# First loads on three queues, constant products ahead of them, and the memory norm behind the first convolution block

## The chip, the core and the metric

The kernel runs on one core of one Trainium2 chip. The metric is the device time of one execution in microseconds (us). The engines are named as in the profile: PE is TensorE (matmuls; PEld is its weight load), DVE VectorE, ACT ScalarE, POOL GpSimd, SP SyncE, which issues most of the transfers.

## What is computed

A model of width 1024 on 512 tokens: a layer with a short convolution, a layer with windowed attention, both with attention to a memory of 256 rows and a gated feed-forward part, and a third block behind them. What the change touches is the beginning of the first layer, cut here from the reference:

```python
def rmsnorm(x, g):
    x32 = x.astype(jnp.float32)
    y = x32 * lax.rsqrt(jnp.mean(x32 * x32, axis=-1, keepdims=True) + EPS)
    return (y * g.astype(jnp.float32)).astype(x.dtype)
...
    mem_n = rmsnorm(mem, mem_norm)
...
        mem_kv = mem_n @ w_mem_kv[i]
        mk, mv = jnp.split(mem_kv, 2, axis=-1)
...
        h = rmsnorm(x, norm_mix[i])
...
            proj = h @ a_w_in[i]
            u, b_gate, c_gate, q_mem = jnp.split(
                proj, [CONV_WIDTH, 2 * CONV_WIDTH, 3 * CONV_WIDTH], axis=-1)
            y_tok = _short_conv(u, b_gate, c_gate, a_conv_w[i])
```

`_short_conv` multiplies `c_gate` with `u`, filters that with three taps along the tokens and multiplies the result with `b_gate`.

## The kernel before, in words

Activations are held with the 1024 features on partitions, as eight chunks of 128 x 512. Every fp32 operand of a product is split into a high part (ScalarE copies it, L70) and a low part (VectorE subtracts, L76 for activations with their gain, L80 for weights), and a product is three matmuls (`mm3`): high by high (L120), low activation by high weight (L121), high activation by low weight (L122). `weights` fetches one block of 128 columns, 512 KB, as `wr`, and splits it into `wh` and `wl`; the first two blocks are fetched, and split, in two halves. There are two `wr` buffers and three each of `wh` and `wl`, so a block's fetch waits until the block two ahead has been split.

The root mean square of a token is one factor per column of the result, so the products begin before it is known: `g` is the chunk times its gain, and the factor `R` is multiplied onto the result. For it ScalarE squares the chunks (`sq`), VectorE adds them up (`acc`), `token_mean` sums over partitions with matmuls on ones (L174), VectorE works out the reciprocal root in a dozen small dependent steps (`m`, `ri`, `rt`, `rz`), and `spread` builds diagonals `dg` (L203) and multiplies them with ones on TensorE (L206) to have the factor on all partitions (`Ra`).

`load_consts` issues the first transfers. The first layer (`layer_a`) then runs convolution block 0 (products `u` and `c` in bank group `pp`, `b` in `lg`), block 1 (`lg`, `lg`, `po`), then `mem_kv`: `mem_rows` fetches the eight memory chunks, squares them, forms `mrs` and `mR` in the manner of `R`, and splits `gm`; two products for keys and the products for values follow. Behind them stand the queries, whose first product (L120 into `pp`) is the first `pp` product after the blocks; then the memory attention and blocks 2 to 5.

Each engine executes its own instructions strictly in order, and so does each queue that issues transfers. That order is set by the framework's scheduler when the kernel is built, from the order of the code and its own estimates of cost. `sink` (twelve numbers for the second layer) is fetched here and negated on VectorE (`negsink`).

## Time and profile before

| | |
|---|---|
| three runs | 1681.52, 1681.77 and 1689.32 us, median 1681.77 |
| the profiled execution | 1686.65 us, its span 1684.9 us |
| mean granted clock of TensorE | 0.987 |
| busy: PE, DVE, ACT, POOL | 1619.6, 1248.2, 756.6, 196.4 us |
| moved by DMA | 171.60 MB |

The span reaches from the first to the last instruction. Times within it count from its start. Starts in a timeline are those of instructions, which overlap: on TensorE the distance from start to start is the pace, not the length given. "[1.64 <-ACT wh L70]" says that the engine stood idle for 1.64 us before the instruction and that ScalarE's write of `wh` ended that. The granted clock is in parts of full speed.

### The profile page before, as it was taken

How to read it: one execution, taken by the hardware profiler on the slowest of the kernel's cores; microseconds unless marked ns; L12 is line 12 of the kernel's file. 1: busy time of each engine (PE TensorE's matmuls, PEld its weight loads, DVE VectorE, ACT ScalarE, POOL GpSimd, SP SyncE). 2: the span in 40 equal slices, each digit the busy share in tenths (PEclk: the TensorE clock that was granted, in tenths of full speed). 3: DMA queues.
4: the chain of work that ended last, by engine and by line, in shares of the span. 5: the costliest groups of instructions: out<-in, count | busy, mean ns of one | idle time of the engine just before them, and what ended most of it. 6: DMA issues, size and time to landing. Idle time of an engine off the chain costs nothing.

```text
span 1684.9 us, 24388 instructions
## 1 busy us (share of the span) xinstructions
PE 1619.6 (96%) x9408; PEld 1415.5 (84%) x9408; DVE 1248.2 (74%) x2330; ACT 756.6 (45%) x1404; POOL 196.4 (12%) x186
## 2 busy tenths in 40 slices
PE   8999999999999699999999999979999999999997
PEld 6887888999999588888889999857788888888887
DVE  7866788787776869877877777579788977764443
ACT  6532244454445467634444444324556533333233
POOL 1112410000000600041000000151001000010010
PEclk9999999999999799999999999989999999999999
DMA  6222222332234522232233233332511122243342
GB/s 199 88 88 88 100 76 100 101 113 101 101 104 123 183 94 77 68 101 88 85 103 113 89 113 98 91 118 86 172 45 57 40 76 92 70 150 113 124 158 88
DMA packets 51572, 171.60 MB, mean 102 GB/s; under 512 B 6680, under 2 KB 6880, under 8 KB 51328
## 3 DMA queue, kind: packets, MB, share of 16 engines
q1 hardware_dynamic: 45504, 151.11, 27.1%
q0 software_dynamic: 5376, 18.82, 3.3%
q8 instruction: 74, 1.21, 0.3%
q14 instruction: 42, 0.34, 0.1%
q10 hardware_dynamic: 576, 0.11, 0.0%
HBM read 160.56 MB, written 11.81 MB: 102 GB/s over the span
## 4 chain that ended last, share of the span: by engine, by line
PE 71%; DVE 15%; DMA 7%; ACT 3%; issue 3%; POOL 1%; SPq 0%; DVEq 0%; ACTq 0%; POOLq 0%
PE pp L122 8%; PE pp L121 8%; PE pp L120 8%; PE lg L120 4%; PE lg L121 4%; PE lg L122 4%; DMA wr<-in_w_gu_dram 3%; DVE wl L80 3%; PE pp L575 3%; PE pp L576 2%; PE pp L577 2%; PE tp L262 2%; PE tp L120 2%; PE tp L121 2%; PE tp L122 2%
## 5 line engine op out<-in xcount | busy, mean ns | idle before, releaser
L70 ACT ACTIVATE wh<-wr 128x1024 fp32r<-128x1024 f32 (+3 forms) x246 | 251.9, 1025 | 371.7 <-PE pp L121 129.1
L80 DVE TENSOR_TENSOR wl<-wr,wh 128x1024 fp32r<-128x1024 f32 (+3 forms) x246 | 305.6, 1243 | 70.1 <-ACT wh L70 68.8
L122 PE MATMUL pp<-g,wl 128*128 128x512 f32 x592 | 235.0, 397 | 11.2 <-DVE wl L80 11.2
L120 PE MATMUL pp<-g,wh 128*128 128x512 f32 x592 | 235.8, 399 | 8.1 <-ACT wh L70 8.1
L121 PE MATMUL pp<-g,wh 128*128 128x512 f32 x592 | 234.1, 396 | 0.2 <-DVE g L76 0.2
L122 PEld LDWEIGHTS pp<-g,wl 128*128 128x128 f32 x592 | 112.2, 189 | 33.7 <-DVE wl L80 13.0
L120 PEld LDWEIGHTS pp<-g,wh 128*128 128x128 f32 x592 | 112.6, 190 | 30.3 <-ACT wh L70 8.9
L121 PEld LDWEIGHTS pp<-g,wh 128*128 128x128 f32 x592 | 112.4, 190 | 21.6 <-DVE g L76 0.9
L70 ACT ACTIVATE s<-s 128x512 fp32r<-128x512 f32 x136 | 85.0, 631 | 62.5 <-DVE s L555 59.7
L120 PE MATMUL tp<-acth,wh 128*128 128x512 f32 x264 | 104.4, 396 | 5.7 <-DVE x L638 3.3
L121 PE MATMUL tp<-actl,wh 128*128 128x512 f32 x264 | 104.0, 394 | 0.0
L122 PE MATMUL tp<-acth,wl 128*128 128x512 f32 x264 | 103.4, 392 | 0.0
L80 DVE TENSOR_TENSOR s<-s,s 128x512 fp32r<-128x512 f32 x136 | 90.3, 685 | 1.9 <-ACT s L70 1.7
L575 PE MATMUL pp<-Bh,s 128*128 128x256 f32 x272 | 77.5, 285 | 3.4 <-ACT g L70 3.4
L575 PE MATMUL lg<-Bh,s 128*128 128x256 f32 x272 | 77.8, 286 | 1.3 <-DVE u L582 1.3
L577 PE MATMUL pp<-Bh,s 128*128 128x256 f32 x272 | 77.4, 285 | 0.3
L577 PE MATMUL lg<-Bh,s 128*128 128x256 f32 x272 | 77.4, 285 | 0.0
L555 DVE TENSOR_TENSOR s<-wr,wr 128x512 f32<-128x512 f32 x68 | 46.8, 688 | 39.7 <-DMA wr<-in_w_gu_dram 39.7
L120 PEld LDWEIGHTS tp<-acth,wh 128*128 128x128 f32 x264 | 50.0, 190 | 16.4 <-ACT wh L70 2.6
L122 PEld LDWEIGHTS tp<-acth,wl 128*128 128x128 f32 x264 | 50.0, 190 | 10.6
L638 DVE TENSOR_TENSOR x<-x,tp 128x512 f32<-128x512 f32 x72 | 49.2, 683 | 12.6 <-PE tp L122 12.6
L576 PE MATMUL lg<-Bl,s 128*128 128x256 f32 x204 | 58.1, 285 | 0.0
(503 smaller groups left out, 4557.5 us busy)
## 6 DMA issues: line engine op xcount, KB each, us to landing
wr<-in_w_gu_dram SPq DMA_DIRECT2D x68, 512.0 KB, 3.8
wr<-in_w_in_dram SPq DMA_DIRECT2D x44, 512.0 KB, 3.5
wr<-in_w_down_dram SPq DMA_DIRECT2D x32, 512.0 KB, 3.7
wr<-in_a_w_in_dram SPq DMA_DIRECT2D x18, 512.0 KB, 3.5
wr<-in_w_down_dram SPq DMA_DIRECT2D x16, 384.0 KB, 3.3
wr<-in_w_gate_dram SPq DMA_DIRECT2D x10, 512.0 KB, 3.5
wr<-in_w_up_dram SPq DMA_DIRECT2D x10, 512.0 KB, 3.4
wr<-in_a_w_out_dram SPq DMA_DIRECT2D x8, 512.0 KB, 3.4
```

The source lines that it names most:

```text
L70: self.nc.scalar.activation(out, in_, AF.Copy, scale=scale)
L80: self.nc.vector.tensor_tensor(out, x, hi.bitcast(F32), op=ALU.subtract)
L120: mm(ps, ah, bh, start=start, stop=False)
L121: mm(ps, ah, bl, start=False, stop=False)
L122: mm(ps, al, bh, start=False, stop=stop)
L262: self.nc.tensor.transpose(ps[:, c:c + 128], src, self.ident)
L555: nc.vector.tensor_tensor(t, a, b, op=ALU.add)
L575: mm(ps, ah, bh, start=start and j == 0, stop=False, skip_group_check=not start)
L576: mm(ps, ah, bl, start=False, stop=False, skip_group_check=not start)
L577: mm(ps, al, bh, start=False, stop=j == 3, skip_group_check=not start)
L638: nc.vector.tensor_tensor(x, x, ps, op=ALU.subtract)
```

## The change

Chunks 4 to 7 of x are issued from GpSimd's queue and the second weight block from ScalarE's; the other first loads stay with SyncE. The fetch of `ident` is written further down. Ten fp32 matmuls of ones by ones (128 x 128) go into a bank of the group `tp`, and `zero` is made from their result times 0 in place of from `ones`. `mem_rows` is called between blocks 0 and 1, and its result is handed to `mem_kv`.

```diff
--- before.py
+++ after.py
@@ -100,7 +100,7 @@
         self.lo_of(lo[:, :n], x, hi[:, :n], scale)
         return hi, lo
 
-    def weights(self, src, nk, nn, parts=1):
+    def weights(self, src, nk, nn, parts=1, eng=None):
 
         nc, n = self.nc, nk * nn
         raw = self.wp.tile([128, 1120], F32, name=self.nm("wr"), tag="wr", bufs=self.wbufs["wr"])
@@ -108,7 +108,7 @@
         lo = self.wp.tile([128, WMAX], F32R, name=self.nm("wl"), tag="wl", bufs=self.wbufs["wl"])
         step = n // parts
         for s in (slice(a, a + step) for a in range(0, n, step)):
-            nc.sync.dma_start(raw[:, s], src[:, s] if parts > 1 else src)
+            (eng or nc.sync).dma_start(raw[:, s], src[:, s] if parts > 1 else src)
         for s in (slice(a, a + step) for a in range(0, n, step)):
             self.copy(hi[:, s], raw[:, s])
             self.lo_of(lo[:, s], raw[:, s], hi[:, s])
@@ -300,15 +300,20 @@
         self.ones = self.const("ones", [128, 128])
         nc.vector.memset(self.ones, 1.0)
         self.zero = self.const("zero", [128, 128], F32R)
-        self.copy(self.zero, self.ones, 0.0)
         nc.scalar.dma_start(self.gains, T["gains"])
-        nc.scalar.dma_start(self.ident, T["ident"])
         self.x = [self.slot("x", name="x") for _ in range(8)]
         nc.sync.dma_start(self.x[0], T["x"][:, 0])
+        for c in range(4, 8):
+            nc.gpsimd.dma_start(self.x[c], T["x"][:, c])
+        ps = self.psum("tp")[:, :128]
+        for i in range(10):
+            nc.tensor.matmul(ps, self.ones, self.ones, start=i == 0, stop=i == 9)
+        self.copy(self.zero, ps, 0.0)
         self.h0 = self.gained(self.x[:1], self.gain(0))
-        self.w0 = [self.weights(T["a_w_in"][i], 8, 128, 2) for i in (0, 12)]
-        for c in range(1, 8):
+        self.w0 = [self.weights(T["a_w_in"][i], 8, 128, 2, e) for i, e in ((0, nc.sync), (12, nc.scalar))]
+        for c in range(1, 4):
             nc.sync.dma_start(self.x[c], T["x"][:, c])
+        nc.scalar.dma_start(self.ident, T["ident"])
         self.conv = self.const("conv", [128, 18])
         nc.scalar.dma_start(self.conv, T["conv"])
         self.sink = self.const("sink", [128, 12])
@@ -369,9 +374,9 @@
             res.append((hi, lo))
         return res
 
-    def mem_kv(self, layer):
+    def mem_kv(self, layer, gm=None):
         nc, T = self.nc, self.T
-        gm = self.mem_rows()
+        gm = gm or self.mem_rows()
         ks = []
         for b in range(2):
             ps = self.psum("lg")[:, :256]
@@ -481,8 +486,9 @@
         h = self.h0 + self.gained(self.x[1:], self.gain(0)[:, 1:])
         _, R = self.norm_row(1e-5, "Ra", True)
         ys = [self.conv_block(0, h, R, "b", self.w0)]
+        gm = self.mem_rows()
         ys.append(self.conv_block(1, h, R, "b", banks=("lg", "lg", "po")))
-        ks, vs = self.mem_kv(0)
+        ks, vs = self.mem_kv(0, gm)
         qs = []
         for b in range(2):
             qs += self.stack_q(self.queries(T["a_w_in"][18 + b], h, R))
```

The scheduler then sets another order. ScalarE at the start of the program, before (`g` and `acc` are of the first x chunk, `wr_93` and `wr_102` the first two weight blocks):

```order
L304 DMA gains<-in_gains_dram 128x64
L70 ACT_TABLE_LOAD
L70 ACTIVATE zero<-ones 128x128
L305 DMA ident<-in_ident_dram 128x128
L70 ACTIVATE g_90<-x_81,gains 128x512
L313 DMA conv<-in_conv_dram 128x18
L70 ACTIVATE wh_94<-wr_93 128x512 x2
L315 DMA sink<-in_b_sinks_dram 128x12
L70 ACTIVATE wh_103<-wr_102 128x512 x2
L159 ACTIVATE acc_145<-x_81 128x512
```

and with the change (`wr_107` and `wr_116` are the two blocks, `tp_92` the bank of the constant products):

```order
L303 DMA gains<-in_gains_dram 128x64
L316 DMA ident<-in_ident_dram 128x128
L111 DMA wr_116<-in_a_w_in_dram 128x512 x2
L70 ACT_TABLE_LOAD
L70 ACTIVATE g_104<-x_79,gains 128x512
L70 ACTIVATE zero<-tp_92 128x128
L70 ACTIVATE wh_108<-wr_107 128x512 x2
L70 ACTIVATE wh_117<-wr_116 128x512 x2
L318 DMA conv<-in_conv_dram 128x18
L320 DMA sink<-in_b_sinks_dram 128x12
L70 ACTIVATE g_135<-x_80,gains 128x512
```

The fetches of the second block are new here, the fetches of `conv` and `sink` stand behind the splitting of both blocks, `ident` is still the second, and the table load stands directly ahead of `g`.

VectorE behind the splitting of the first block, before (`g` with its three operands is the low half of a chunk):

```order
L80 TENSOR_TENSOR wl_95<-wr_93,wh_94 128x512 x2
L80 TENSOR_TENSOR wl_104<-wr_102,wh_103 128x512 x2
L317 TENSOR_SCALAR negsink<-sink 128x12
L76 SCALAR_TENSOR_TENSOR g_124<-x_82,gains,g_124 128x512
L76 SCALAR_TENSOR_TENSOR g_127<-x_83,gains,g_127 128x512
L166 TENSOR_TENSOR acc_145<-acc_145,sq_147 128x512
L76 SCALAR_TENSOR_TENSOR g_130<-x_84,gains,g_130 128x512
```

and with the change:

```order
L80 TENSOR_TENSOR wl_109<-wr_107,wh_108 128x512 x2
L80 TENSOR_TENSOR wl_118<-wr_116,wh_117 128x512 x2
L76 SCALAR_TENSOR_TENSOR g_135<-x_80,gains,g_135 128x512
L76 SCALAR_TENSOR_TENSOR g_138<-x_81,gains,g_138 128x512
L322 TENSOR_SCALAR negsink<-sink 128x12
L76 SCALAR_TENSOR_TENSOR g_141<-x_82,gains,g_141 128x512
L76 SCALAR_TENSOR_TENSOR g_144<-x_83,gains,g_144 128x512
```

`negsink` has moved behind the first two low halves, and the adds of the squares behind all of the low halves.

TensorE in block 1, before (`lg_299` is its product `u`, `dg_193` the first norm's diagonals):

```order
L122 MATMUL lg_299<-g_133,wl_304 128x512
L120 MATMUL lg_299<-g_136,wh_303 128x512
L121 MATMUL lg_299<-g_136,wh_303 128x512
L206 MATMUL tp_198<-dg_193,ones 128x512
L122 MATMUL lg_299<-g_136,wl_304 128x512
L120 MATMUL lg_299<-g_139,wh_303 128x512
L121 MATMUL lg_299<-g_139,wh_303 128x512
```

and with the change, from the end of block 0 on (`lg_393` and `lg_394` are block 1's `u` and `c`, `tp_341` takes the memory's means):

```order
L122 MATMUL lg_215<-g_153,wl_275 128x512
L120 MATMUL lg_393<-g_104,wh_397 128x512
L121 MATMUL lg_393<-g_104,wh_397 128x512
L120 MATMUL lg_394<-g_104,wh_429 128x512
L121 MATMUL lg_394<-g_104,wh_429 128x512
L206 MATMUL tp_209<-dg_204,ones 128x512
L174 MATMUL tp_341<-ones,acc_318 128x2 x2
L122 MATMUL lg_393<-g_104,wl_398 128x512
L120 MATMUL lg_393<-g_135,wh_397 128x512
```

The spread product of the first norm stood behind 17 matmuls of block 1 and stands behind four now, and the memory's means follow at once, where they came behind the whole of block 1. The memory norm's own spread product now stands behind the third matmul of block 1's last product, `po`; before it stood in the products for the memory's keys and values.

## Rows read from the trace of the kernel before

**Rows 1.** The page, first part: busy us, share of the span and instructions by engine.
```profile
PE 1619.6 (96%) x9408; PEld 1415.5 (84%) x9408; DVE 1248.2 (74%) x2330; ACT 756.6 (45%) x1404; POOL 196.4 (12%) x186
```

**Rows 2.** Stretches: length, busy us by engine (count), granted clock, DMA share, GB/s.
```profile
55.70:59.00 3.30, 3.30 (x14) 3.12 (x15) 2.56 (x5) 1.60 (x4) 0.00 (x0) 0.50 0.72 259
571.00:588.00 17.00, 7.42 (x21) 6.23 (x22) 14.28 (x29) 3.52 (x5) 8.95 (x13) 0.50 0.60 215
```

**Rows 3.** DMA view, 0 to 20 us: 40 slices; issues: queue, count, KB, us to landing.
```profile
DMA  0005689999798999999999998898998997899972
GB/s 0 0 0 49 175 202 323 320 321 314 258 299 295 397 387 387 322 362 395 392 403 394 402 369 311 254 381 340 246 291 336 328 213 197 262 369 385 361 283 107
...
gains<-in_gains_dram ACTq DMA_DIRECT2D x1, 32.0 KB, 3.5
...
sink<-in_b_sinks_dram ACTq DMA_DIRECT2D x1, 6.0 KB, 5.4
```

**Rows 4.** Timeline of TensorE: start, us, line, operation, tiles, count, idle time before and releaser.
```profile
9.19 0.80 PE L120 MATMUL pp<-g,wh 128*128 128x512 f32 x1 [1.64 <-ACT wh L70]
...
14.10 0.63 PE L122 MATMUL pp<-g,wl 128*128 128x512 f32 x1
14.53 0.49 PE L120 MATMUL pp<-g,wh 128*128 128x512 f32 x1
...
22.60 0.39 PE L120 MATMUL lg<-g,wh 128*128 128x512 f32 x1
22.83 0.39 PE L121 MATMUL lg<-g,wh 128*128 128x512 f32 x1
```

**Rows 5.** Timeline of ScalarE, 0 to 10 us.
```profile
1.18 1.28 ACT L70 ACT_TABLE_LOAD   x1 [1.18 <-PEq L1287]
...
4.27 0.72 ACT L70 ACTIVATE g<-x,gains 128x512 fp32r<-128x512 f32 x1 [1.49 <-DMA gains<-in_gains_dram]
...
5.22 1.31 ACT L70 ACTIVATE wh<-wr 128x512 fp32r<-128x512 f32 x2 [0.22 <-DMA wr<-in_a_w_in_dram]
...
8.51 1.15 ACT L70 ACTIVATE wh<-wr 128x512 fp32r<-128x512 f32 x2 [1.99 <-DMA wr<-in_a_w_in_dram]
```

**Rows 6.** Timeline of VectorE, 11 to 33 us.
```profile
11.34 0.17 DVE L317 TENSOR_SCALAR negsink<-sink 128x12 f32<-128x12 f32 x1 [0.88 <-DMA sink<-in_b_sinks_dram]
...
13.36 2.07 DVE L76 SCALAR_TENSOR_TENSOR g<-x,gains,g 128x512 fp32r<-128x512 f32 x3
...
25.25 0.42 DVE L166 TENSOR_TENSOR acc<-acc,sq 128x256 f32<-128x256 f32 x1
25.59 0.16 DVE L183 TENSOR_SCALAR ri<-m 128x4 int32<-128x4 int32 x1
25.66 0.48 DVE L76 SCALAR_TENSOR_TENSOR gm<-mem,gains,gm 128x256 fp32r<-128x256 f32 x1
26.06 0.17 DVE L184 TENSOR_SCALAR ri<-ri 128x4 int32<-128x4 int32 x1
...
27.42 1.22 DVE L80 TENSOR_TENSOR wl<-wr,wh 128x1024 fp32r<-128x1024 f32 x1
...
31.93 0.87 DVE L203 TENSOR_SCALAR dg<-ident,rz 128x128 f32<-128x128 f32 x4
```

**Rows 7.** Chain that ended last, 0 to 64 us: start, us, what.
```profile
24.35 0.79 PE tp L174 x8
...
33.01 0.97 PE tp L206 x2
```

**Rows 8.** Timeline of TensorE, 55 to 63 us.
```profile
55.63 1.20 PE L206 MATMUL tp<-dg,ones 128*128 128x256 f32 x2 [2.46 <-DVE dg L203]
...
57.06 0.41 PE L142 MATMUL lg<-wh,gm 128*128 128x256 f32 x1
57.27 0.41 PE L143 MATMUL lg<-wh,gm 128*128 128x256 f32 x1
...
63.00 0.40 PE L120 MATMUL pp<-g,wh 128*128 128x512 f32 x1
```

## The prediction

> **What bounds the kernel now.** I read the page first, then the stretches, then the first 64 us engine by engine, because every instruction that the change moves stands there; behind the first query product (63.00 us, [rows 8]) the order of every engine is the same as before. TensorE is busy 96% of the span [rows 1], so time is won only where it idles, or where its clock is at the lower of its two levels. [Rows 2] are two stretches at a granted clock of 0.50, the 1.2 GHz level: one right behind the memory norm, one far behind the change. From [rows 3] the reader is to see that the first loads fill the chip's DMA engines: 0.8 to 0.9 busy and more from about 3 us on, with nearly all of it from one queue. [Rows 4] are TensorE's start: the second weight block is first used at 9.19, behind 1.64 us of idleness; 512-column matmuls follow each other by 0.43 us (14.10 to 14.53) and later by 0.23 (22.60 to 22.83). A pitch of 0.43 is that of the lower level: in the slow stretch of [rows 2] 256 columns take 0.21 [rows 8]. [Rows 5] and [rows 6] show how ScalarE and VectorE prepare those operands in order, [rows 7] the products of the first norm (its means, then the product that spreads it), [rows 8] the wait of 2.46 us for the memory norm and the slow products behind it.
>
> **The change, part by part.** I follow one number, the start of the first query product, 63.00 us. After it nothing changes but the offset.
>
> *Ten constant products.* The spread product of 512 columns takes 0.97 us at the full clock [rows 7]; a quarter of it, 0.24, is one of the ten, 0.49 at the half clock. Ten are 2.4 to 4.9 us. They start near 1 us (when the ones are written, the first thing that VectorE does) and end at 3.4 to 6. TensorE's first real matmul cannot start before the first `wh` half, 5.22 + 0.65 = 5.87 [rows 5]; so on TensorE itself they cost nothing. `zero` now waits for them, on ScalarE, ahead of `wh`. The activation table load (1.28) ran at 1.18, before anything had landed; now it waits for the x chunk with the `g` behind it, so it starts about where `g` did, 4.27. ScalarE's first `wh` is therefore some 1.3 us later plus about 0.3 for `zero`: 6.8 in place of 5.22, and the first matmul near 7.5. The cover is the idleness ahead of 9.19: 7.5 + 3 x 0.43 = 8.8. Cost 0; were the second block there at once, up to 1.6.
> What they can gain is the clock. The six matmuls from about 12 to 14.5, the last slow ones [rows 4], would save 0.2 each, 1.2 us, if the clock rose earlier and stayed. But between the tenth product and about 12 us TensorE has some eight matmuls of work, so idle stretches like the 1.64 us of [rows 4] stay. I take 0; the other end is -1.2.
> The Trainium skill, "TensorE: Matmul & The Clock Gate", Part 1, says that the throttled state is the default, that activity releases it and that idleness brings it back. By its first half alone the sum would be 1.2 us lower, by the second the 0 stands; the slow stretch right behind the idle 2.46 us [rows 2, 8] speaks for the second.
>
> *Three queues.* The same bytes are fetched. Issue times change: the second block's two loads go out at about 1.5 to 2 us from ScalarE's queue, x chunks 4 to 7 at about 2 to 4 us (an estimate: as early as their queues come to them) from GpSimd's, where SyncE issued them one behind the other, last of the eight. Yet the DMA engines are full [rows 3], and the four x chunks (1 MB) now move beside the second weight block (0.5 MB) instead of behind it. Before, ScalarE had the block from 8.51 on [rows 5] and took its two halves in 1.15, so the last half was there by 9.0. At some 300 GB/s [rows 3] 1 MB takes 3.5 us; depending on how much of it gets in ahead, the last half comes 0.3 to 4 us later than before. I take 11.0, +2. The x chunks are all there by 13, which buys little, since ScalarE takes them in order behind `wh` of that block.
> The Trainium skill, "DMA: Bandwidth & Descriptors", section "Queues, rings and completion order", says that every DMA engine takes turns between the queue rows that have work. By it three queues share the same 16 engines, x chunks delay the weight block and the +2 stands; if a queue kept the engines until it is empty, the block, issued first, would land no later than before. The trace of before, with one large queue, cannot show which.
>
> *The sink.* `sink` is issued on ScalarE behind the last `wh` half of the second block, 11.0 + 0.65, so near 12, and takes 3.5 (the row of `gains`) to 5.4 (its own) [rows 3]: it lands at 15.5 to 17.4. VectorE works in order, and `negsink` stands now behind the first two of the seven low halves of `g`; before, issued some 6 us earlier, it cost 0.88 of waiting [rows 6]. VectorE is through with what stands ahead (two `wl` halves, two low halves of 0.69) near 13.2 and then waits 2 to 4 us. Five low halves (5 x 0.69 = 3.5 [rows 6]) are queued behind it, and TensorE waits for them, since the products of the third and later chunks need them. TensorE itself, at the half clock, has 12 matmuls ahead of that point (10.2 + 12 x 0.43 = 15.4), so a wait until 15 is covered. With the sink at 15 the b product, which began at 22.60, begins at 23 to 25; at 17.4 at 26 to 27; with an early sink at 22.5. I take 24.8: **+2.2**, ends -0.1 and +4.4.
>
> *First norm beside block 1.* The means stand behind five matmuls of the b product, 5 x 0.23 = 1.2 us from its start, and take 0.8 [rows 7]. From there VectorE needs, until `dg` is done, 5 adds of 0.34, 7 low halves of 0.40, 11 small steps of 0.07 (starts in [rows 6]: 25.25, 25.59, 25.66, 26.06) and 0.87 for `dg`: 1.7 + 2.8 + 0.8 + 0.9 = 6.2 us; before, with two `wl` of 1.22 among them, it was 25.25 to 32.80, 7.5. So `dg` is ready 1.2 + 0.8 + 6.2 + 0.1 = 8.3 us behind the start of b. TensorE used to meet its spread product in mid-block; now it does after four matmuls of block 1: 24 x 0.23 + 0.8 + 4 x 0.23 = 7.2. A new wait of 1.1. The next `wl` (a low half, then 1.22) hides behind the spread product and the memory means but for 0.1: **+1.2**, ends 0.6 and 2.1.
>
> *Memory norm.* Before: TensorE waits 2.46 us, then runs at the half clock: 14 records from 55.7 to 59 [rows 2], each 0.1 longer than at the full clock, and a spread product of 1.20 [rows 8] against half of 0.97. 2.46 + 1.4 + 0.7: 4.5 us hang on that spot. Now the means are taken at the start of block 1, and the spread stands after three matmuls of its last product, some 10 us later. Its chain runs on VectorE between four `wl` (1.22), the conv taps, `b`, `u` and `v` (0.7 each): about 12 us of work. So the wait does not vanish; I take 2.0 left, and no slow stretch behind it, since 512-column products follow at once: -0.5 - 1.4 - 0.7, and -0.4 as the first norm is earlier for the conv chain on which VectorE hangs here: **-3.0**, ends -4.5 and -0.5.
>
> Sum: +2.2 + 1.2 - 3.0 = +0.4 us. The profiled execution took 1686.65 us (span 1684.9 and 1.75 around it), 4.9 above the median, so this one would become 1687.0; against the median of the three runs, 1681.77, it is 1682.2. By the ends: -0.1 + 0.6 - 4.5 - 1.2 = -5.2 and 4.4 + 2.1 - 0.5 = +6.0. Besides, an offset moves every idle stretch against the clock: from 571 to 588 us it was at 0.50 [rows 2], with 7.4 us of matmuls that take half as long at the full clock. A stretch like it longer or shorter by a third is 1.2 us either way.
>
> **Rivals.** *All of it works* (15%): the clock stays up from the constant products (-1.2), the sink is early, the memory wait is covered entirely (-4.5), the first norm costs its 1.2: -4.5 us, 1677.3. For it: the loads are issued earlier. Against: the DMA engines have no room [rows 3].
> *The sink blocks VectorE* (16%): issued behind a block that lands at 12 or later, it lands after 17; from about 15 on, each further microsecond holds five low halves, and TensorE by up to as much. The memory norm gives back only 0.5: 4.4 + 1.2 - 0.5 = +5.1, 1686.9, slower. For it: `negsink` waited already with an issue 6 us earlier [rows 6]. Against: at the half clock TensorE is late anyway.
> *The loads change nothing* (14%): bytes arrive as before and the sink is early enough; only the norms count: 1.2 - 3.0 = -1.8, 1680.0.
> My forecast, a loss at the start that the memory norm gives back, has 55%.
>
> **How the numbers follow.** A measurement of this kernel can tell some 0.5%, 8.4 us, from no change. No case reaches that; only a slow stretch lost or added elsewhere could carry the first rival (3%) or the second (5%) past it. So faster 0.03, same 0.92, slower 0.05. The range takes in the middles of the rivals: 1677.5 to 1687.0.
>
> **What would show it.** In the profile of the changed kernel: ten products done by 6 us and a pitch of 0.43 again at 10 to 13; the second block's `wh` later than 8.51; `negsink` waiting for the sink by 2 us or more, until 15 to 17; the b product at 24.8; a wait of TensorE for `dg` of about 1.1 in block 1 and one near 2 in its last product, with no slow stretch behind it; the first query product at 63.4. Wrong it would be if the b product starts before 22.6 or after 27, if no wait for `dg` is left, or if time changes behind 65 us by over 3 us.

## The result, and the profile after

The changed kernel took 1693.21 us (median of ten runs, 1689.29 to 1699.53) where the kernel before took 1683.71 (ten runs, 1681.39 to 1689.32): a ratio of 1.0057, 95% interval 1.0039 to 1.0075. It is slower by about 9.5 us, outside the forecast's range; in this comparison that is over 0.5%, to which the forecast gave 5%. Two more comparisons of the same two kernels, told of below, gave ratios of 1.0040 (1.0023 to 1.0057) and 1.0049 (1.0035 to 1.0063). All three say slower; the size lies between some 5 and 10 us, because both kernels scatter by 8 to 10 us from run to run. The profiled executions stand closer, 1689.29 after and 1686.65 before: one from the quick end of its kernel's runs, the other from the slow end of its own. So the profiles serve for where things stand, not for the difference in time.

TensorE is as busy as before; only the twenty records of the ten products are new (first part of the page, answering to [rows 1]):

```profile
PE 1621.2 (96%) x9428; PEld 1415.0 (84%) x9428; DVE 1249.0 (74%) x2330; ACT 757.1 (45%) x1404; POOL 195.7 (12%) x190
```

TensorE's timeline of the first 66 us of the changed kernel shows the ten products, every real start that the forecast named, and the number that it followed (answers to [rows 4] and [rows 8]):

```profile
1.06 4.63 PE L310 MATMUL tp<-ones 128*128 128x128 f32 x20 [1.06 <-DVE ones L301]
6.87 0.79 PE L120 MATMUL pp<-g,wh 128*128 128x512 f32 x1 [1.17 <-ACT wh L70]
...
9.07 0.79 PE L120 MATMUL pp<-g,wh 128*128 128x512 f32 x1 [0.56 <-ACT wh L70]
...
12.91 1.22 PE L120 MATMUL pp<-g,wh 128*128 128x512 f32 x2 [2.19 <-ACT g L70]
...
18.73 0.51 PE L121 MATMUL pp<-g,wh 128*128 128x512 f32 x1 [1.24 <-DVE g L76]
...
26.39 0.39 PE L120 MATMUL lg<-g,wh 128*128 128x512 f32 x1
...
35.20 1.12 PE L206 MATMUL tp<-dg,ones 128*128 128x512 f32 x2 [0.97 <-DVE dg L203]
...
49.09 0.70 PE L206 MATMUL tp<-dg,ones 128*128 128x256 f32 x2 [1.40 <-DVE dg L203]
...
65.93 0.40 PE L120 MATMUL pp<-g,wh 128*128 128x512 f32 x1
```

The products end at 5.7, as forecast, and the first real matmul stands at 6.87 behind `zero`. The second block is used at 9.07, about as before (9.19). From there on the forecast is off: TensorE waits 2.19 us for `g` of the second chunk, 1.24 for a low half, and b, the third product of block 0, begins at 26.39 in place of 22.60. The two waits for `dg` are there, 0.97 and 1.40 us (forecast 1.1 and 2), with no slow stretch behind the second. The query product begins at 65.93: +2.93 us, forecast +0.4.

ScalarE's timeline tells why `g` is late (answers to [rows 5]):

```profile
4.12 1.28 ACT L70 ACT_TABLE_LOAD   x1 [4.12 <-DMA x<-in_x_dram]
...
6.04 0.26 ACT L70 ACTIVATE zero<-tp 128x128 fp32r<-128x128 f32 x1
6.20 1.14 ACT L70 ACTIVATE wh<-wr 128x512 fp32r<-128x512 f32 x2
8.39 0.63 ACT L70 ACTIVATE wh<-wr 128x512 fp32r<-128x512 f32 x1 [1.06 <-DMA wr<-in_a_w_in_dram]
10.77 0.63 ACT L70 ACTIVATE wh<-wr 128x512 fp32r<-128x512 f32 x1 [1.75 <-DMA wr<-in_a_w_in_dram]
...
11.18 0.46 ACTq L320 DMA_DIRECT2D sink<-in_b_sinks_dram  x1
12.14 0.72 ACT L70 ACTIVATE g<-x,gains 128x512 fp32r<-128x512 f32 x1 [0.73 <-DMA x<-in_x_dram]
14.05 2.62 ACT L70 ACTIVATE g<-x,gains 128x512 fp32r<-128x512 f32 x4 [1.19 <-DMA x<-in_x_dram]
```

The table load waits for the chunk, `zero` comes out before `wh`, the block's second half is read at 10.77. The second and third of the eight chunks are read as they land, at 12.14 and 14.05. Before, ScalarE read these two in one go from 10.09 on, and the very last at 15.08:

```profile
10.09 1.32 ACT L70 ACTIVATE g<-x,gains 128x512 fp32r<-128x512 f32 x2
...
15.08 0.73 ACT L70 ACTIVATE g<-x,gains 128x512 fp32r<-128x512 f32 x1 [0.19 <-DMA x<-in_x_dram]
```

VectorE after the change (answers to [rows 6]):

```profile
17.84 0.17 DVE L322 TENSOR_SCALAR negsink<-sink 128x12 f32<-128x12 f32 x1 [2.29 <-DMA sink<-in_b_sinks_dram]
17.92 3.40 DVE L76 SCALAR_TENSOR_TENSOR g<-x,gains,g 128x512 fp32r<-128x512 f32 x5
```

`negsink` waits 2.29 us for `sink`, until 17.84, and all five remaining low halves stand behind it. The DMA view of the same 20 us (answers to [rows 3]):

```profile
DMA  0002699899999999999999999989899999986200
...
x<-in_x_dram SPq DMA_DIRECT2D x4, 256.0 KB, 8.7
x<-in_x_dram POOLq DMA_DIRECT2D x4, 256.0 KB, 7.4
...
wr<-in_a_w_in_dram ACTq DMA_DIRECT2D x2, 256.0 KB, 7.7
...
sink<-in_b_sinks_dram ACTq DMA_DIRECT2D x1, 6.0 KB, 6.6
```

The engines are as full as before, from about 2.5 us on; each transfer only takes longer, 7.4 and 8.7 us for a chunk and 7.7 for a half of the second block. `sink` took 6.6. Before, all of these but `sink` were on one queue, and took:

```profile
x<-in_x_dram SPq DMA_DIRECT2D x8, 256.0 KB, 5.0
wr<-in_a_w_in_dram SPq DMA_DIRECT2D x4, 256.0 KB, 5.3
```

### The profile page after: what moved, and what is told of

It reads as the page before. It is cut to its first block, busy times and chain, and to the rows that moved or that the text cites. A ratio compares the mean times of both kernels' runs of the same rounds, so it can differ in the third digit from the quotient of the medians.

```text
span 1687.5 us, 24429 instructions
## 1 busy us (share of the span) xinstructions
PE 1621.2 (96%) x9428; PEld 1415.0 (84%) x9428; DVE 1249.0 (74%) x2330; ACT 757.1 (45%) x1404; POOL 195.7 (12%) x190
## 4 chain that ended last, share of the span: by engine, by line
PE 58%; DVE 13%; DMA 7%; ACT 3%; issue 2%; POOL 1%; DVEq 0%; ACTq 0%; SPq 0%; POOLq 0%
PE pp L122 6%; PE pp L120 6%; PE pp L121 6%; DMA wr<-in_w_gu_dram 4%; PE pp L581 2%; PE pp L582 2%; PE pp L583 2%; PE lg L120 2%; DVE wl L80 2%; PE lg L121 2%; PE lg L122 2%; PE tp L262 2%; PE tp L120 2%; PE tp L121 2%; PE tp L122 2%
## 5 line engine op out<-in xcount | busy, mean ns | idle before, releaser
L122 PEld LDWEIGHTS pp<-g,wl 128*128 128x128 f32 x592 | 112.2, 190 | 34.0 <-DVE wl L80 13.5
L582 PE MATMUL pp<-Bl,s 128*128 128x256 f32 x204 | 57.7, 283 | 0.0
```

Of the source, the lines that this page charges most:

```text
L122: mm(ps, al, bh, start=False, stop=stop)
L582: mm(ps, ah, bl, start=False, stop=False, skip_group_check=not start)
```

## The experiments

All are timed against the kernel before on the chip that they ran on. "Query" is the start of the first query product in the one profile (before 63.00), b that of block 0's product b (before 22.60), "median" the difference of the medians to the kernel before in the same runs. The starts are of one execution each: the query product of the change lies between 65.26 and 67.60 in its three profiles, that of e9 at 60.79 and 61.19 in two, so a difference of a microsecond or two between two rows can be chance. In e14 the means of the first norm stand ahead of b, elsewhere behind it. The ratio isn't that of the two medians; where they differ, as in e15 and e16, it is the interval that tells.

| version | b | query | median, us | ratio and interval |
|---|---|---|---|---|
| e1 products alone | 23.71 | 65.84 | +2.8 | 1.0022 (1.0007 to 1.0037) |
| e2 queues alone | 27.12 | 67.89 | +5.2 | 1.0038 (1.0025 to 1.0050) |
| e3 norm alone | 23.29 | 62.18 | -1.3 | 0.9993 (0.9981 to 1.0004) |
| e4 change without products | 27.83 | 66.92 | +2.4 | 1.0021 (1.0007 to 1.0035) |
| e5 change again | 28.50 | 67.60 | +5.5 | 1.0040 (1.0023 to 1.0057) |
| e6 change, sink later | 24.91 | 64.08 | +4.3 | 1.0027 (1.0013 to 1.0041) |
| e7 change, x on one queue | 23.82 | 62.91 | +1.5 | 1.0010 (0.9998 to 1.0022) |
| e8 norm, sink later | 22.20 | 61.04 | -2.8 | 0.9981 (0.9970 to 0.9993) |
| e9 norm, sink on GpSimd | 21.78 | 60.79 | -3.0 | 0.9978 (0.9967 to 0.9989) |
| e10 e9 with products read by zero | 23.14 | 65.42 | +2.0 | 1.0017 (1.0006 to 1.0028) |
| e11 e4 with sink later | 27.32 | 66.42 | +3.0 | 1.0013 (1.0003 to 1.0023) |
| e12 change, third time | 25.70 | 65.26 | +8.3 | 1.0049 (1.0035 to 1.0063) |
| e13 e9 with ten idle products | 22.94 | 61.90 | +0.9 | 1.0009 (0.9992 to 1.0025) |
| e14 e9 with 24 idle products | 23.95 | 60.94 | -3.3 | 0.9986 (0.9974 to 0.9998) |
| e15 e9 again | 22.18 | 61.19 | -1.6 | 0.9997 (0.9985 to 1.0010) |
| e16 e9 with one product read by zero | 22.67 | 61.73 | -3.0 | 0.9992 (0.9979 to 1.0005) |

### The parts alone: e1, e2, e3, e4

e1 takes the products and `zero` from the change, e2 the queues and the place of `ident`, e3 the call of `mem_rows`; e4 is the change without the products.

```diff
 e1, against the kernel before
-        self.copy(self.zero, self.ones, 0.0)
...
+        ps = self.psum("tp")[:, :128]
+        for i in range(10):
+            nc.tensor.matmul(ps, self.ones, self.ones, start=i == 0, stop=i == 9)
+        self.copy(self.zero, ps, 0.0)
 e3, against the kernel before
-    def mem_kv(self, layer):
+    def mem_kv(self, layer, gm=None):
...
-        gm = self.mem_rows()
+        gm = gm or self.mem_rows()
...
+        gm = self.mem_rows()
         ys.append(self.conv_block(1, h, R, "b", banks=("lg", "lg", "po")))
-        ks, vs = self.mem_kv(0)
+        ks, vs = self.mem_kv(0, gm)
```

> The kernel before with the ten constant products and zero made from them, nothing else moved in the code. Two theories of the 9.5 us between the medians. Offset theory: what the change costs is the later start of the first query product (65.93 in the profile after, 63.00 before, +2.9), and the rest is how the clock happens to fall in single runs; the products cost nothing of that offset, so the query product is within 1 us of 63.0 and the time within 2 us of the kernel before. Clock theory: activity of TensorE from 1 us on changes where the clock falls in the rest of the program; then the query product is near 63 as well, but the median is 5 to 7 us above the kernel before.

> The kernel before with the x chunks 4 to 7 on GpSimd's queue, the second weight block on ScalarE's and the fetch of ident further down; no constant products, memory norm where it was. Offset theory: the second block and the sink land late, the product b of block 0 starts near 26 in place of 22.6, the query product near 66.5, time +3 to +4 us. Clock theory: the same offset, and no more than it: +3 to +4, where the products bring the other 6.

> The kernel before with the memory norm called between the blocks and nothing else. Both theories: the start is as before, TensorE waits about 1 us for the first norm's diagonals and 1.4 for the memory norm's, without a slow stretch behind the latter; query product 61.5 to 62, time -1 to -2 us. If the memory norm itself brings longer slow stretches later, the median is above the kernel before.

> The changed kernel without the constant products (zero made from ones as before). Offset theory: query product 65 to 66, time +2 to +3 us against the kernel before. Clock theory: +2 to +3 as well, that is 6 to 7 us below the changed kernel, and the mean granted clock of its runs as before (0.987).

Both theories missed e1: the kernel with the products alone does start the query product later, by 2.84. VectorE's timeline says how (e1, 8 to 16 us):

```profile
9.42 0.17 DVE L320 TENSOR_SCALAR negsink<-sink 128x12 f32<-128x12 f32 x1 [4.88 <-DMA sink<-in_b_sinks_dram]
```

With the products in the code the scheduler put the fetch of `sink`, and its negation, ahead of everything that has to wait, and VectorE stood for 4.88 us at `negsink`, ahead of the first low half of `g`; the memory norm's wait is 3.1 us then, with a stretch at the lower clock behind it. e2 is the dear part, as its b of 27.12 shows. (In e2 and e4 the scheduler put the second fetch of the second block behind a `wh` on ScalarE, which the change does not; so their start is later than that of the queues alone would be.) The norm is the only one that gains: -0.8 at the query product, as its TensorE timeline has it (e3). Its b is 0.7 later than before, though the order up to there is the same, so from b on the norm gains 1.5:

```profile
62.18 0.40 PE L120 MATMUL pp<-g,wh 128*128 128x512 f32 x1
```

In all four, the median moves as the query product does, within 1.5 us: +2.8 against +2.8, +5.2 against +4.9, -1.3 against -0.8, +2.4 against +3.9. The parts' medians add up to +6.7, but each part was given an order of its own by the scheduler, so this isn't a sum of the change's own pieces.

### Which wait makes the start late: e6, e7; the change again: e5, e12

e6 moves the fetch and the negation of `sink` behind the first layer, e7 puts all x chunks back on SyncE's queue.

```diff
 e6, against the change
-        nc.scalar.dma_start(self.sink, T["b_sinks"].to_broadcast([128, 12]))
...
-        nc.vector.tensor_scalar(self.negsink, self.sink, -1.0, None, op0=ALU.mult)
...
         self.layer_a()
+        self.nc.scalar.dma_start(self.sink, self.T["b_sinks"].to_broadcast([128, 12]))
+        self.nc.vector.tensor_scalar(self.negsink, self.sink, -1.0, None, op0=ALU.mult)
 e7, against the change
-        for c in range(4, 8):
-            nc.gpsimd.dma_start(self.x[c], T["x"][:, c])
...
-        for c in range(1, 4):
+        for c in range(1, 8):
             nc.sync.dma_start(self.x[c], T["x"][:, c])
```

> The changed kernel as it is, once more, on the chip that runs the next three. The single parts gave medians of +2.8 (products), +5.2 (queues) and -1.3 us (norm), each within 0.6 us of the shift of its first query product (+2.8, +4.9, -0.8). Offset theory: the first comparison's +9.5 came from few runs of a kernel that scatters over 10 us; here the median is +2 to +5 above the kernel before, as the query product's shift of +2.9 says. Clock theory: the three parts together cost what none of them costs alone, and the median is again +7 or more.

> The changed kernel with the fetch of sink and its negation written behind the first layer. If VectorE's wait for sink (2.29 us, until 17.84) is what makes the start late, the low halves follow without it and the product b starts 1 to 2 us earlier than in the change (about 24.6 to 25.4 in place of 26.4), the query product near 64.5: +1.5 us against the kernel before, and 1.5 below the change. If the late x chunks (12.1 and 14.05 on ScalarE) set the pace, it gains under 0.5.

> The changed kernel with all x chunks back on SyncE's queue in their order; the second weight block stays on ScalarE's. If the four chunks on GpSimd's queue took their share of the DMA engines ahead of chunks 1 and 2, then here ScalarE gets these earlier (10.5 and 11.5 in place of 12.1 and 14.05), the product b starts at 23 to 24, the query product at 62.5 to 63.5, time -0.5 to +0.5 us against the kernel before. If the DMA engines are the bound whatever the queue, b starts at 26 as in the change, +3.

> The changed kernel once more, to lie beside the three runs above on the same chip. Comparisons so far: +9.5 and +5.5 us of median, with query products at 65.93 and 67.60 in the two profiles. If the offset is all there is, +3 to +5; if there is a further cost behind 66 us, +6 to +9.

Moving `sink` takes 1.9 us off the query product of the first profile (64.08 against 65.93; against all three of the change, 65.93, 67.60 and 65.26, it is 1.2 to 3.5). Moving the chunks back takes 3.0 (2.4 to 4.7), and here is how, in ScalarE's and TensorE's timelines of e7:

```profile
10.48 4.40 ACT L70 ACTIVATE g<-x,gains 128x512 fp32r<-128x512 f32 x7 [0.26 <-issue]
```

```profile
23.82 0.39 PE L120 MATMUL lg<-g,wh 128*128 128x512 f32 x1
...
62.91 0.40 PE L120 MATMUL pp<-g,wh 128*128 128x512 f32 x1
```

All seven chunks come off ScalarE without a break from 10.48 on, where the change waited until 14.05 for the third. The block's second half is read at 9.59 and `sink`, issued 1.2 us earlier, costs 1.32 of waiting in place of 2.29. So the late chunks, with what follows from them, are the larger half of the late start: four chunks that are needed last, on a queue of their own, moved on the same DMA engines beside the two that were needed next.
The Trainium skill, "DMA: Bandwidth & Descriptors", section "Queues, rings and completion order", has each DMA engine take turns between the queue rows with work; the longer landings on all three queues agree with it. The rate shows that the further queues added none (the 20-us view moves 5.71 MB before and 5.73 after), and what the turns do to the order of landing is what e7 shows.

The clock is a third part, in one of the three profiles. In e5 the granted clock was full from 10.2 to 13.6 us and at the lower level from there to 23.8, where it was full from 14.7 on before, from 17.1 on in the first profile and from 16.0 on in e12. TensorE in e5, behind its wait for the low halves:

```profile
18.31 0.79 PE L121 MATMUL pp<-g,wh 128*128 128x512 f32 x1 [1.11 <-DVE g L76]
18.91 0.63 PE L122 MATMUL pp<-g,wl 128*128 128x512 f32 x1
...
23.17 0.63 PE L120 MATMUL pp<-g,wh 128*128 128x512 f32 x1
```

These matmuls follow each other by 0.43 us, where the first profile has 0.23 from 19.07 on. Added up over the matmuls ahead of b, the slow pitch cost 3.2 us before, 3.0 and 3.0 in the first profile and e12, and 5.6 in e5: that is why its b, at 28.50, is the latest of all.

### A version without its waits, with and without the products: e8 to e11

e8 is e3 with `sink` moved as in e6; e9 does that on GpSimd's queue and engine, so that VectorE and ScalarE have nothing to do with it; e10 is e9 with the products of the change; e11 is e6 without the products.

```diff
 e9, against e3
-        nc.scalar.dma_start(self.sink, T["b_sinks"].to_broadcast([128, 12]))
...
-        nc.vector.tensor_scalar(self.negsink, self.sink, -1.0, None, op0=ALU.mult)
...
         self.layer_a()
+        self.nc.gpsimd.dma_start(self.sink, self.T["b_sinks"].to_broadcast([128, 12]))
+        self.nc.gpsimd.tensor_scalar(self.negsink, self.sink, -1.0, None, op0=ALU.mult)
```

> The kernel before with the memory norm behind the first block, and with sink fetched and negated behind the first layer; queues and start as before. The norm alone gave -0.8 at the query product and -1.3 in the median; without the wait for sink (0.70 there) the low halves start 0.7 earlier, but TensorE is at the half clock then and has work, so another 0 to -0.5: query product 61.7 to 62.2, time -1 to -2 us.

> The kernel before with the memory norm behind the first block and with sink fetched and negated on GpSimd, so that no wait for it stands on VectorE or ScalarE. The version with sink on VectorE but later started the query product at 61.04 and its median was 2.8 us below the kernel before; here the same, query product 61 to 61.5, time -2 to -3 us. It is the pair of the next run.

> The run above with the ten constant products added. If the products cost nothing by themselves (alone they cost 2.8, but VectorE then waited 4.88 us for sink), the first matmul is later by 1 us, the product b within 0.7 us of the run above, time 0 to +1 us against it, so -1 to -3 against the kernel before. If activity from 1 us on costs in the rest of the program, the median is 2 to 5 us above the run above though the query product is not.

> The changed kernel without the constant products and with sink fetched and negated behind the first layer: queues and norm alone. The change without products had its query product at 66.92 and a median of +2.4, the change with sink later 64.08 and +4.3. Here about 64.5 to 65.5 and, if the offset is all there is, +1.5 to +2.5 us; if the products bring a cost of their own, this lies 2 to 4 us below the change with sink later (+4.3) with the same query product.

e8 and e9 lie 2.8 and 3.0 us below the kernel before in the median, clear of the noise (both intervals end below 1); e9 once more (e15) lies 1.6 below, with an interval that holds 1. So the gain is likely, and its size is not settled. e10 is 5.0 above e9, and its query product shows where, 4.6 later. TensorE, e10:

```profile
31.97 0.50 PE L122 MATMUL lg<-g,wl 128*128 128x512 f32 x1 [1.37 <-DVE wl L80]
...
46.96 1.11 PE L206 MATMUL tp<-dg,ones 128*128 128x256 f32 x2 [2.70 <-DVE dg L203]
...
65.42 0.40 PE L120 MATMUL pp<-g,wh 128*128 128x512 f32 x1
```

The start is late by 1.4 at b, then TensorE waits 1.37 for a low weight in block 1 and 2.70 for the memory norm, and a stretch at the lower clock follows (47.0 to 50.5 us). e11 missed: without the products, and with `sink` off the path, b stands at 27.32, because here too the second fetch of the second block stands behind a `wh`, and that half is read at 13.49.

### Activity or order: e13 to e18

e13 keeps the ten products but leaves `zero` as before, so that nothing waits for them and the order of ScalarE and SyncE is that of e9 (on VectorE one add and one low half of the memory norm, behind 22 us, changed places); e14 does so with 24; e16 has one product, read by `zero`; e15 is e9 again, e17 and e18 are e13 again for the profile.

```diff
 e13, against e9
         nc.sync.dma_start(self.x[0], T["x"][:, 0])
+        ps = self.psum("tp")[:, :128]
+        for i in range(10):
+            nc.tensor.matmul(ps, self.ones, self.ones, start=i == 0, stop=i == 9)
```

> The best version so far (norm behind block 0, sink on GpSimd; query product 60.79) with the ten products put ahead on TensorE and nothing waiting for their result: zero is made from ones as before, so the order on every other engine is that of the version without them. With the products read by zero, the query product came at 65.42, 4.6 later, and the clock was full from 6.1 to 9.5, at the lower level until 16.3. Clock theory: it is the activity that moves the clock's rise behind the start of the real work; here it rises at 16 or later too, query product 62 to 65, time +2 to +4 us against the version without. Order theory: what costs is the order on ScalarE and VectorE that follows from zero's wait; here the query product stays at 60.8 to 61.5 and the time within 1 us of the version without.

> As the run before, with 24 products in place of ten, which last until about 9.4 us, when the second weight block is there. They delay the first three matmuls from 5.9 to 9.4. Clock theory: no idle stretch is left before the real work, so a clock that rose near 6 stays up, the pitch is 0.23 from 9.4 on, and TensorE is limited by the low halves of g alone: product b 21 to 22, query product 60 to 60.8, time 0 to -1.5 us against the version without products. If it falls all the same in the wait for chunks at 10 to 12, the rise comes at 16 as with ten: +2.

> The version without products once more, the pair of the three other runs on this chip: query product 60.5 to 61.5, time -2 to -4 us against the kernel before; between its two profiles the query product should differ by under 0.7 us, where the change's three lie between 65.26 and 67.60.

> As the run before, with a single product, and zero read from its result: the dependence of the change with a tenth of its activity. Clock theory: query product and time as the version without, within 1 us. Order theory: as the version with ten products read by zero, +2 to +5 us.

> The version with ten products that nothing waits for, once more, for its profile. Its median lay 2.4 us above its pair, its query product only 0.7 to 1.1. If the start differs from one execution to the next (the clock falls and rises again at other times), the query product here is not at 61.9 but up to 3 us later or earlier; if it is within 0.3 of 61.9 again, the further 1.5 us or so lie behind 66 us.

> The same for a third profile: start that differs, query product away from 61.9 by over 0.5 in at least one of the three; start that repeats, all three within 0.3.

TensorE in e13 (starts, and in the brackets the waits):

```profile
1.06 4.60 PE L310 MATMUL tp<-ones 128*128 128x128 f32 x20 [1.06 <-DVE ones L301]
5.84 0.50 PE L120 MATMUL pp<-g,wh 128*128 128x512 f32 x1 [0.19 <-ACT wh L70]
6.17 0.40 PE L121 MATMUL pp<-g,wh 128*128 128x512 f32 x1
...
9.08 0.80 PE L120 MATMUL pp<-g,wh 128*128 128x512 f32 x1 [2.02 <-ACT wh L70]
9.67 0.63 PE L121 MATMUL pp<-g,wh 128*128 128x512 f32 x1
10.10 0.63 PE L122 MATMUL pp<-g,wl 128*128 128x512 f32 x1
```

The first three matmuls follow by 0.33 to 0.40 us, better than 0.43: the clock is up (in its record from 5.5 us on). Nothing is gained by these three, since TensorE is idle behind them. Then 2.02 us of idleness, and the pitch is 0.43 again (9.67 to 10.10); the record has the lower level from 8.9 until 15.7 (e17: 14.7, e18: 14.8), where e9's clock rose at 13.5 and e15's at 14.2. So the products made the clock rise early, for nothing, and if anything later for the real work. The cost is small: query product 61.90, 61.34 (e17) and 61.40 (e18) against 60.79 and 61.19. (By the mark set for e17 and e18 the start does differ between executions of one kernel, by 0.6.) With 24 products the clock is up from 4.0 to 10.8 and still falls behind a wait of 2.20 for the second chunk; the slow pitch then costs 1.5 us ahead of b in place of e9's 2.4, but the first real matmul starts at 7.84 in place of 5.80. e14's median lies 1.7 below that of e15, its interval overlaps, and the two cannot be told apart. So the order theory explains most of e10's 4.6 us (a `zero` that waits, and with it another place for the table load, the splitting and the small fetches), and the products' own time on TensorE explains none of it: the first real matmul stands at 5.84 in e13 and 5.80 in e9. That the dependence on one product (e16) costs little, 0.5 to 0.9 at the query product, says the same: there the scheduler left the rest as it was, but for the place of `ident`. In the change itself the products' price can't be read off, because e4, the change without them, got another order again.

**What stays open.** The change's query product moves by 2.3 to 4.6 us, its median by 5.5 to 9.5. In the nine versions without the ten products (e14 counted among them), the median's move less the query product's is -1.7 to +0.3; in those with them -0.4 to +3.2, and for the change itself +6.6, +0.9 and +6.1. That sets a median of many runs against a start seen in one, so the profiles are the better witness: from the query product to the end the change's three take 1621.6, 1628.1 and 1626.4 us, and the one of the kernel before 1621.9. The order there is the same in all. And it isn't simply work on TensorE at the start, since e14, with 24 products, has -1.2. What could carry it is the stretch at the lower clock near 1110 us, which was longer than 13 us in six of ten profiles with ten products (e1, e5, e7, e10, e13, e17) and in one of ten without (e15); of the 6.2 us that e5 has more than the kernel before behind the query product, 4.9 arise there, but of e12's 4.6 only 1.1. Its length is decided by something that differs between executions of one kernel. e17 and e18 are the same kernel, their query products 0.06 us apart, their spans 1684.4 and 1678.0. Matmul by matmul they are within 1.0 us of each other up to 1100 us (0.4 at the end of it), and 6.3 apart at 1150. TensorE at the end of that wait, e17 and then e18:

```profile
1118.83 0.80 PE L122 MATMUL pp<-g,wl 128*128 128x512 f32 x1 [12.57 <-DVE wl L80]
```

```profile
1116.10 0.79 PE L122 MATMUL pp<-g,wl 128*128 128x512 f32 x1 [10.21 <-DVE wl L80]
```

Behind it, the stretch from 1120 to 1131 us (length, busy us by engine, granted clock), e17 and then e18:

```profile
1120.00:1131.00 11.00, 11.00 (x36) 9.29 (x35) 6.48 (x30) 1.06 (x1) 0.00 (x0) 0.51 0.36 110
```

```profile
1120.00:1131.00 11.00, 11.00 (x54) 9.01 (x54) 8.08 (x36) 2.25 (x3) 1.03 (x1) 0.97 0.48 145
```

And what made the wait, the adds of squares on VectorE that run beside GpSimd's own add, e17 and then e18, each with GpSimd's add beside the first of them:

```profile
1109.49 2.35 DVE L76 SCALAR_TENSOR_TENSOR acc<-sq,g,acc 128x512 f32<-128x512 f32 x1 [0.93 <-POOL sq L157]
1110.01 1.27 POOL L166 TENSOR_TENSOR acc<-acc,sq 128x512 f32<-128x512 f32 x1
...
1114.04 2.35 DVE L76 SCALAR_TENSOR_TENSOR acc<-sq,g,acc 128x512 f32<-128x512 f32 x1 [0.93 <-POOL sq L157]
```

```profile
1109.12 0.75 DVE L76 SCALAR_TENSOR_TENSOR acc<-sq,g,acc 128x512 f32<-128x512 f32 x1 [0.93 <-POOL sq L157]
1109.64 1.36 POOL L166 TENSOR_TENSOR acc<-acc,sq 128x512 f32<-128x512 f32 x1
...
1112.48 0.75 DVE L76 SCALAR_TENSOR_TENSOR acc<-sq,g,acc 128x512 f32<-128x512 f32 x1 [0.93 <-POOL sq L157]
```

Each such add takes 0.75 us or 2.35, and these two were long in e17 and short in e18; the adds ahead of them have the same lengths in both. Long or short, these adds start 0.50 to 0.52 us ahead of GpSimd's, in all profiles, so what decides between the two lengths can't be seen. 54 matmul records fit behind in e18 where 36 did in e17. That scatter of 6 us inside one kernel is shown. It goes with the clock: among the 27 to 35 runs of the kernel before on each of four chips, the longer a run, the lower its mean granted clock (correlation -0.76 to -0.90). That ten products at the start weight it, some 1100 us later, is only counted, six of ten against one of ten, with the mark of 13 us set after the fact, and no run shows a way in which they could.
The Trainium skill, "SBUF — State Buffer", section "SBUF: two separate sides", describes the pair of ports that VectorE and GpSimd share as a lock held for a whole instruction by whichever starts first. The two lengths of the same add are of that kind: the long one is 1.6 us longer, and GpSimd's add beside it takes 1.27 to 1.31. That the first to start has the pair isn't borne out by these, since VectorE's add starts first whether it is long or short; where GpSimd's starts first, by 0.12 to 0.53 us, VectorE's is lengthened in all 40 cases, to 1.71 to 2.35.

## Why the prediction was wrong

Two steps failed. The first is in the part on the three queues, that the x chunks are "all there by 13, which buys little": the second and third came late, and with them the start, by more than the +2.2 that the forecast laid to `sink` alone. That accounts for a query product later by 2.3 to 4.6 us. The second is "After it nothing changes but the offset", with 1.2 us either way for one stretch: behind the query product the medians hold another 0.9 to 6.6 us, and the cause of that part stays open.

- **Ten products, cost 0.** Right for their own time: they ran from 1.06 to 5.7 in the shadow of the loads, and e13 with its two repeats puts their price, where the order stays as it was, at 0.2 to 1.1 us. Wrong for what reads them: the scheduler's new order that came with it cost 4.6 us at the query product in e10. In the forecast that stood as "Cost 0; were the second block there at once, up to 1.6".
- **What the clock gains, taken as 0.** No gain came, but a loss had no place in the forecast: in e5 the early rise was followed by the lower level until 23.8, which cost 2.6 us more slow pitch than the first profile has; in the other two profiles the term is near 0.
- **Three queues, second block's last half at 11.0.** Read at 10.77 in the profile, 10.06 and 10.22 in the others: nearly right. But the step on the chunks failed: the third chunk was read at 14.05, 13.21 and 13.51 in the three profiles, against about 10.7 before. The forecast counted bytes up to the last chunk and not which chunk lands when. The chunks at the head of SyncE's queue shared the DMA engines with those of GpSimd's. e7 prices it at 3.0 us at the query product (2.4 to 4.7), a term that the sum lacked.
- **The sink.** Landing at 15.5 to 17.4, waiting 2 to 4 us: measured 17.84 and 2.29, a price of 1.9 by e6 (1.2 to 3.5). It was issued earlier than forecast, at 11.18, and took 6.6 us in place of 3.5 to 5.4. The mechanism was right, and for a sink at 17.4 the forecast had b at 26 to 27, where it came (26.39); the +2.2 was the middle of its range. All in all the start cost +3.8, +5.9 and +3.1 at b, the 5.9 with the slow clock of e5. That b of 28.50 is beyond 27, one of the forecast's own signs of being wrong.
- **First norm beside block 1, +1.2.** The wait of 1.1 came as 0.97.
- **Memory norm, -3.0.** The wait left is 1.40 where 2.0 was taken, and no slow stretch follows. By the starts of the products the spot cost 4.3 us before (6.26 us from 52.90 to 59.16 for work of 1.9 at the full clock) and 1.75 in the change, a gain of 2.6. From b to the query product the change takes 39.54, 39.10 and 39.56 us against 40.40, so the two norms together are worth -0.8 to -1.3 and not -1.8 (e3: -1.5), and the first norm, by what is left in the first profile, costs about 1.7. That no slow stretch followed was luck as far as the reason goes: "since 512-column products follow at once" is refuted by e10, where they followed a wait of 2.70 us and ran at a pitch of 0.43 from 48.29 to 50.42.
- **The rivals.** The losing one had the place (VectorE held up by `sink`) and, with +5.1, nearly the size of the change's smallest median; it was given 16%, and 5% to slower by over 0.5%. The nearness is chance: the block landed before 12, and the memory norm gave back more than its 0.5. The rival that gains had none of its conditions, and the one in which the loads change nothing fails by the late chunks.
- **The range.** Its upper end allowed +5.2 over the median of three runs that it started from, 1681.77; over the ten runs of the comparison, 1683.71, it is +3.3. The median came out at +5.5 to +9.5. Of that, 3.3 (mean of three) are in the first 66 us; the rest is what stays open above. The forecast's last sign of being wrong was "if time changes behind 65 us by over 3 us": by the medians it does in two of the three comparisons, in the profiles in e5 and e12 (+6.2 and +4.6) and not in the first (-0.3).

## What to carry to other kernels

When loads already fill the DMA engines, another queue did not make them faster here (286 and 287 GB/s), it reordered them: give the engines first what is needed first, and a queue of its own only to what nobody waits for soon. A wait that is hoisted into an in-order engine (a constant of twelve numbers, 4.88 us in e1) holds up all that stands behind it, so fetch and prepare what is needed late on an engine that has nothing to do then: that, with the norm moved, is the version that did best (e9, -3.0 us of median, and -1.6 in a second comparison that can't be told from 0). Products that warmed the clock were followed by an idle stretch here, and the clock was down again behind it (2.02 us in e13, 2.20 in e14). And read the new order, not the diff: in four of the versions (e1, e2, e4, e11) the place that the scheduler gave to a fetch set the start.

## What the runs showed that I had not expected

- The memory norm's wait of TensorE was 2.46 to 3.11 us in four profiles (before, e1, e2, e10), and a stretch at the lower clock followed in each; it was 1.38 to 1.75 in all others, and none followed. This is no rule for other places: in the profile of the kernel before a wait of 2.16 us ends at 1110.11 and the clock falls at 1110.4, in that of the change the same wait ends at 1113.35 and the clock stays up.
- Two executions of one kernel differ by 6 us: two adds beside GpSimd's take 2.35 us in one and 0.75 in the other, and the stretch at the lower clock there is 20.5 or 10.3 us long.
- A median over few runs of this kernel is worth +-3 us: the kernel before had 1683.71 in ten runs, and 1687.49, 1685.79, 1686.79 and 1686.89 in 27 to 35 runs each, on four chips. No run tells the chips from the scatter.
